# A hybrid decoder layer on one core: split weight pieces of the input projection kept in DRAM between its two passes

## The chip, the cores and the metric

The kernel runs on one core of one Trainium2 chip. The metric is the device time of one execution in microseconds (us); a version's time is the median of several executions. A profile is one execution with the hardware profiler on. Engines are named as in its rows: PE is TensorE (matmuls; PEld its weight loads), DVE is VectorE, ACT is ScalarE, POOL is GpSimd, and SP is the engine whose in-order queue issues the DMA transfers. The granted clock (PEclk) is given in parts of TensorE's full speed, 2.4 GHz.

## The reference, cut to what matters

One layer over a sequence of 2048 tokens with 1024 features. All of x is normalised and multiplied by one matrix `w_in` of 1024 x 4096; its columns feed three groups of heads, whose outputs are concatenated, multiplied by `w_out` (1536 x 1024), normalised and added to x.

```python
hn = rms_norm(x, g_pre)
proj = hn @ w_in                                  # (2048, 1024) @ (1024, 4096)
rg_x, rg_g, da_q, da_k, da_v, da_g, xa_q, xa_g = jnp.split(proj, cuts, axis=-1)

xc = causal_depthwise_conv(rg_x, conv_w, conv_b)  # width 4 along the sequence
y_rg = rg_lru(xc, w_rg_a, b_rg_a, w_rg_x, b_rg_x, lru_lambda) * silu(rg_g)

o = diff_attention(q, k, v, lam)                  # 4 heads, causal, two softmaxes each
y_da = rms_norm(o, g_subln) * (1.0 - LAMBDA_INIT) * silu(da_g)

km, vm = split(rms_norm(mem, g_mem) @ w_mem_kv)   # 256 memory tokens
y_xa = mem_cross_attention(xa_q, km, vm) * silu(xa_g)

y = concatenate([y_rg, y_da, y_xa]) @ w_out
x = x + rms_norm(y, g_post)
```

## The kernel before

Everything is fp32. For its matmuls a tensor is split into a high part (the value rounded to a matmul format) and a low part (what the rounding left), and each product is three matmuls: high x high, low x high, high x low (`mm3`). A weight is split by `split_weight`: ACT casts the raw piece to the high half (L237), then POOL subtracts that from the raw piece to get the low half (L238).

**The projection.** The sequence is cut into four chunks of 512 tokens, and the 4096 columns of `w_in` into 16 pairs of 256 (`PAIRS`): `qk` (query and key of a head), `v`, `g` (gates), `xa` (memory attention) and `rg` (the recurrent group). `project()` runs twice. The first pass goes over chunks 0 and 1, the second over chunks 2 and 3 with the pairs in the order `ORDER_B`. A pair has four steps u, one for each chunk and half of the pair; a step is a sum of 24 matmuls over 8 blocks kb of the contraction. The `ip` tiles of the profile are the results of these steps.

**The weight pieces.** The weight of a pair comes in four pieces, each for two blocks kb: raw 128 x 512 (256 KB, `wraw`), split 128 x 1024 (512 KB, `wp`). Raw pieces have three buffers, split ones six (`pw`). Pieces are numbered in the order of use: 0 to 7 and 24 to 79 for the first pass, 8 to 23 for the memory tokens' weight `w_mem`, 80 to 143 for the second pass. `w_load(i)` issues the transfer of a raw piece on SP (L316), `w_conv(i)` splits it and issues `w_load(i + 3)`. While a pair runs, `project()` converts the first two pieces of the next pair in its steps 0 and 1, and the other two in step 3, after the blocks 1 and 3, since each of these takes over the buffer of a piece whose last matmul has just been given out. So in the second pass all of `w_in` is read and split once more.

**The rest.** The queries, keys, values and gates of the attention go through DRAM: `ev_qk` and its like store them (`QD`, `KD`, `VD`, `GD`), and the attention loads them back (`q` L645, `kv` L608 and L621, `gt` L775). The softmax streams run between the projection's matmuls; in them DVE and POOL scale the exponentials `e` by the row sums (L719, L718), PE transposes the result (`pt`), and ACT and DVE split it (`pthl`, L759, L760). The group outputs wait in DRAM (`YD`) for the output projection (`po`). For an `rg` pair, `ev_rg` runs the convolution on DVE (`xc`, L550, L553), casts it to a high half (`xchl`, L556, DVE) and subtracts for the low half (L557, POOL); the gates' matmuls (`rgo`) read both. Then `rg_gates` runs the recurrence (a scan on DVE, L590).

**What sets the order.** PE's order is written out by the program: a clock of its own (`now`, `pump`, `spawn`) hands out the attention's matmuls between those of the projection. DVE, ACT and POOL get their order from a scheduler with priorities. SP's queue is in order: an issue that waits for its buffer or its data holds every later one back. `store(fn, delay)` spawns an issue that much later on the program's own clock.

Of the kernel before, what the change touches and what calls it, by code (L numbers as in the profile page):

```python
# [9 lines left out]
F32 = mybir.dt.float32  # L10
# [39 lines left out]
ORDER_B = (0, 12, 2, 13, 1, 14, 3, 15, 4, 8, 6, 9, 7, 10, 11, 5)  # L50
# [7 lines left out]
def hybrid_layer(  # L58
# [13 lines left out]
    nc = tc.nc  # L72
# [14 lines left out]
    dr = ctx.enter_context(tc.tile_pool(name="dr", bufs=1, space=bass.MemoryType.DRAM))  # L87

    def f4(name, shape=(128, 1024), dt=F32, pool=p4):
        return pool.tile(list(shape), dt, tag="f4", name=name)  # L90
# [19 lines left out]
    def asf(ap):  # L110
        return ap.bitcast(F32)
# [4 lines left out]
    KD = [[dr.tile([2, 2, 64, CH], F32, name=f"KD{h}{c}") for c in range(NCH)] for h in range(4)]  # L116
    VD = [[dr.tile([128, 2, 4, 128], F32, name=f"VD{h}{c}") for c in range(NCH)] for h in range(4)]
    GD = [[dr.tile([128, CH], F32, name=f"GD{h}{c}") for c in range(NCH)] for h in range(4)]
    KMD = dr.tile([4, 128, 1024], F32, name="KMD")
    YD = [[dr.tile([4, 128, 4, 128], F32, name=f"YD{g}{c}") for c in range(NCH)] for g in range(3)]  # L120

# [82 lines left out]
    def spawn(gen, delay=0.0):  # L204
        streams.append([now[0] + delay, gen])

    def store(fn, delay):

        def go():
            fn()  # L210
            return
            yield
        spawn(go(), delay)
# [22 lines left out]
    def split_weight(raw, hi, lo, eng=nc.gpsimd):  # L236
        nc.scalar.copy(hi, raw)  # L237
        eng.tensor_sub(lo, raw, asf(hi))  # L238
# [65 lines left out]
    def pair_pieces(ps):  # L304
        return [w_in[4 * p + i] for p in ps for i in range(4)]

    wsrc = (pair_pieces(range(2)) + [w_mem[i] for i in range(16)] + pair_pieces(range(2, 16))
            + pair_pieces(ORDER_B))
    MEM0 = 8
    wraw, wcv = {}, {}  # L310

    def w_load(*ids):
        for i in ids:
            if i < len(wsrc):
                wraw[i] = praw.tile([128, 512], F32, tag="raw", name="wraw")
                nc.sync.dma_start(wraw[i], wsrc[i])  # L316

    def w_conv(*ids, eng=nc.gpsimd, pool=pw):
        for i in ids:
            if i < len(wsrc) and i not in wcv:  # L320
                w = wcv[i] = f4("wp", (128, 2, 2, 256), F32R, pool)
                split_weight(wraw.pop(i), w[:, 0].rearrange("p a b -> p (a b)"),
                             w[:, 1].rearrange("p a b -> p (a b)"), eng)
                w_load(i + 3)


    def load_rows(src, n, name):
# [21 lines left out]
    stored = set()  # L349
    setup()  # L350
    w_load(0)
    xr0 = load_rows(x, 4, "xrow")
    w_load(1, 2)
    xb = bigt("xrows", (128, 4, 2, 512), F32)
    xr1 = [[xb[:, i, j, :] for j in range(2)] for i in range(4)]
# [3 lines left out]
    for row in xr0:  # L359
        norm_rows([row], nc.vector)  # L360
    w_conv(0, eng=nc.vector)
    new_hnT(0)
    for _ in transpose_norm(xr0, hnT[0], V_GPRE):
        pass
    ready.add(0)
    w_conv(1, 2, 3, eng=nc.vector)

    def prep_mem():
# [9 lines left out]
    def store_km(i, ts):  # L378
        for j, t in enumerate(ts):
            nc.sync.dma_start(KMD[i + j], asf(t).rearrange("p a b -> p (a b)"))  # L380

    def memory_branch():
# [6 lines left out]
        for p in range(4):  # L389
            i0 = MEM0 + 4 * p  # L390
            if p == 2:
                vmh = f4("vmh", (128, 2, 512), F32R)
                vml = f4("vml", (128, 2, 512), F32R)
            for half in range(2):
                o = ps_m("kv", (128, 256))
                for kb in range(KB):
                    w = wcv[i0 + kb // 2]
                    if p < 2:
                        cs = slice(half * 128, half * 128 + 128)
                        mm3(o, w[:, 0, kb % 2, cs], w[:, 1, kb % 2, cs],  # L400
                            memT[0][:, kb, :], memT[1][:, kb, :], kb == 0, kb == KB - 1)
                    else:
                        tk = slice(half * 128, half * 128 + 128)
                        mm3(o, memT[0][:, kb, tk], memT[1][:, kb, tk], w[:, 0, kb % 2, :], w[:, 1, kb % 2, :],
                            kb == 0, kb == KB - 1)
                    if half == 1 and kb in (1, 3):
                        w_conv(i0 + 6 + kb // 2, eng=nc.vector if kb == 1 else nc.gpsimd)
                    pump()
                if p < 2:
                    hi, lo = kmh[:, 2 * p + half, :], kml[:, 2 * p + half, :]  # L410
                else:
                    cs = slice((p - 2) * 256, (p - 2) * 256 + 256)
                    hi, lo = vmh[:, half, cs], vml[:, half, cs]
                nc.scalar.copy(hi, o)
                nc.vector.tensor_sub(lo, o, asf(hi))
                if half == 0:
                    w_conv(i0 + 4, eng=nc.vector)
                    w_conv(i0 + 5)
                elif p % 2:
                    store(lambda i=p - 1, ts=(kmh, kml) if p == 1 else (vmh, vml): store_km(i, ts), 4.0)  # L420
# [34 lines left out]
    def ev_g(hp, c, half, o):  # L455
        t = f2("gs", (128, CH))
        sigmoid(t, o)
        nc.vector.tensor_mul(t, o, t)
        store(lambda: nc.sync.dma_start(GD[2 * hp + half][c], t), 4.0)

# [4 lines left out]
    def load_km():  # L465
        for i, n in enumerate(("kmh", "kml", "vmh", "vml")):
            t = state[n] = f4(n, (128, 4, 256) if i < 2 else (128, 2, 512), F32R)
            nc.sync.dma_start(asf(t).rearrange("p a b -> p (a b)"), KMD[i])

# [256 lines left out]
    def t_stream(jobs):  # L726

        for h, pr in jobs:
# [45 lines left out]
            c, j = divmod(pr, 2)  # L774
            nc.sync.dma_start(gt, GD[h][c][:, j * 256:j * 256 + 256])  # L775
            nc.scalar.copy(A[:, 0, :], o)
# [23 lines left out]
    def project(chunks, i0, order, hooks, head=False):  # L800
# [5 lines left out]
        for p, u in steps:  # L806
# [27 lines left out]
            for t, kb, ot, wh, wl, xh, xl in mms:  # L834
                mm3(ot, wh, wl, xh, xl, kb == 0, kb == KB - 1)
                if u == 3 and t == (kind == "v"):
                    if first:
                        if kb % 2 and (p == 0 or kb < 4):
                            w_conv(MEM0 + 4 * p + kb // 2)
                    elif kb in (1, 3):  # L840
# [209 lines left out]
```

## Time and profile before

| | |
|---|---|
| median of 3 runs | 1487.29 us (1485.58 to 1488.57) |
| profiled execution | 1490.95 us, its span 1489.1 us |
| busy in the span | PE 95%, PEld 81%, DVE 62%, ACT 54%, POOL 38% |
| mean granted clock | 0.986 |
| SP's DMA queue | 182.64 MB |
| largest group of PE | `ip` matmuls, 676.8 us for the 128x512 form |

The span is counted from the profiled execution's first instruction to its last; its own time is 1.85 us more than that. The busy shares are means over stages. By the first and last instructions of the `ip` groups, the first pass lies at about 0 to 540 us, the second at 540 to 1106, and the output projection after it.

### The profile page before, as it was taken

To read this page: it belongs to the slowest core of one execution; us is meant where nothing else is said; L and a number is where in the kernel's file an instruction comes from. 1 tells how busy PE (TensorE), PEld (TensorE's weight loads), DVE (VectorE), ACT (ScalarE), POOL (GpSimd) and SP (SyncE) were. 2 spreads that over 40 slices of the span, in tenths; PEclk is the share of its full clock that TensorE was granted. 3 is DMA by queue.
4 is the path that set the end of the run, shared out by engine and by line. 5 is a ranking of instruction groups with operands and counts; after the bars stand their busy time and mean duration, and the time that the engine had idled before them with its cause. 6 is when DMAs were issued, how large, how long until landed. Compare 5 with 4: busy or idle time off the path is not lost.

```text
span 1489.1 us, 21951 instructions
## 1 busy us (share of the span) xinstructions
PE 1422.1 (95%) x7568; PEld 1208.6 (81%) x7568; DVE 918.4 (62%) x1862; ACT 811.5 (54%) x1972; POOL 563.8 (38%) x634
## 2 busy tenths in 40 slices
PE   5999999999998899899998999999999999999997
PEld 4789889888886678787786898888877888888886
DVE  6332565677545776757648576767778777777222
ACT  6343545666458674755556555666566545554221
POOL 2231433443446543535425343423346433334221
PEclk9999999999999899999999999999999999999999
DMA  6666666342322146244222543221375234322231
GB/s 218 162 214 219 177 172 206 99 132 82 106 68 64 50 128 187 72 151 123 84 68 71 163 141 128 68 85 40 116 237 174 86 133 151 103 96 76 99 123 70
DMA packets 138655, 184.05 MB, mean 124 GB/s; under 512 B 11440, under 2 KB 81200, under 8 KB 138544
## 3 DMA queue, kind: packets, MB, share of 16 engines
q1 hardware_dynamic: 138400, 182.64, 39.6%
q8 instruction: 59, 0.97, 0.3%
q14 instruction: 52, 0.43, 0.1%
q10 hardware_dynamic: 144, 0.01, 0.0%
HBM read 125.99 MB, written 56.62 MB: 123 GB/s over the span
## 4 chain that ended last, share of the span: by engine, by line
PE 74%; DVE 8%; ACT 6%; POOL 5%; issue 4%; DMA 2%; SPq 0%; DVEq 0%; POOLq 0%; ACTq 0%
PE ip L197 35%; PE po L197 17%; PE s L197 7%; PE o L197 6%; PE pt L201 4%; DVE e L719 2%; PE xas L197 2%; PE kv L197 1%; POOL e L718 1%; PE xao L197 1%; POOL wp L238 1%; DMA wraw<-in_w_in_dram 1%; PE rgo L197 1%; DVE xc L553 1%; ACT e L695 1%
## 5 line engine op out<-in xcount | busy, mean ns | idle before, releaser
L197 PE MATMUL ip<-hnT,wp 128*128 128x512 f32 x2688 | 676.8, 397 | 4.9 <-DVE rgg L563 4.9
L197 PEld LDWEIGHTS ip<-hnT,wp 128*128 128x128 f32 x2688 | 499.0, 190 | 105.8 <-DVE rgg L563 6.1
L695 ACT ACTIVATE e<-s,nm 128x512 f32<-128x512 f32 (+3 forms) x320 | 200.0, 625 | 233.4 <-DVE nm L693 216.3
L238 POOL TENSOR_TENSOR wp<-wraw,wp 128x512 fp32r<-128x512 f32 x133 | 182.2, 1380 | 201.8 <-ACT wp L237 192.8
L693 DVE TENSOR_REDUCE nm<-s 128x1 f32<-128x512 f32 (+3 forms) x320 | 193.2, 605 | 32.4 <-PE s L197 27.7
L197 PE MATMUL po<-wout,yg 128*128 128x512 f32 x768 | 193.5, 393 | 4.2 <-POOL wout L238 1.9
L718 POOL TENSOR_SCALAR e<-e,f 128x512 f32<-128x512 f32 (+3 forms) x160 | 120.3, 767 | 171.1 <-DVE f L714 93.5
L197 PE MATMUL s<-kv,q 128*128 128x512 f32 (+3 forms) x640 | 182.8, 367 | 1.0 <-ACT e L695 0.9
L197 PEld LDWEIGHTS po<-wout,yg 128*128 128x128 f32 x768 | 141.3, 188 | 34.3 <-POOL wout L238 3.3
L719 DVE SCALAR_TENSOR_TENSOR e<-e,f 128x512 f32<-128x512 f32 (+3 forms) x160 | 142.7, 919 | 28.5 <-POOL e L718 28.3
L197 PE MATMUL o<-pthl,kv 128*128 128x256 f32 (+1 forms) x864 | 136.3, 293 | 2.0 <-DVE pthl L760 2.0
L760 DVE TENSOR_TENSOR pthl<-pt,pthl 128x512 fp32r<-128x512 f32 (+1 forms) x144 | 94.6, 657 | 70.4 <-ACT pthl L759 70.0
L197 PEld LDWEIGHTS s<-kv,q 128*128 128x128 f32 x640 | 114.6, 189 | 21.8 <-ACT e L695 1.3
L197 PEld LDWEIGHTS o<-pthl,kv 128*128 128x128 f32 x864 | 116.1, 192 | 5.6 <-DVE pthl L760 2.8
L238 POOL TENSOR_TENSOR yg<-yraw,yg 128x512 fp32r<-128x512 f32 x48 | 64.2, 1341 | 133.1 <-ACT yg L237 122.0
L237 ACT CAST wp<-wraw 128x512 fp32r<-128x512 f32 x144 | 88.2, 618 | 43.9 <-PE ip L197 22.1
L759 ACT CAST pthl<-pt 128x512 fp32r<-128x512 f32 (+1 forms) x144 | 80.8, 561 | 53.3 <-PE pt L201 52.7
L197 PE MATMUL ip<-wp,hnT 128*128 128x256 f32 x768 | 99.4, 284 | 0.0
L197 PE MATMUL po<-wo,yg 128*128 128x512 f32 x384 | 97.3, 392 | 0.0
L197 PEld LDWEIGHTS ip<-wp,hnT 128*128 128x128 f32 x768 | 96.2, 192 | 1.2
L201 PE MATMUL pt<-ident,e 128*128 128x128 f32 x544 | 84.4, 276 | 5.6 <-DVE pthl L760 5.6
L201 PEld LDWEIGHTS pt<-ident,e 128*128 128x128 f32 x544 | 67.9, 142 | 20.8 <-DVE pthl L760 6.0
(183 smaller groups left out, 1731.2 us busy)
## 6 DMA issues: line engine op xcount, KB each, us to landing
wraw<-in_w_in_dram SPq DMA_DIRECT2D x128, 256.0 KB, 2.7
q<-QD SPq DMA_DIRECT2D x128, 128.0 KB, 3.3
kv<-KD SPq DMA_DIRECT2D x24, 512.0 KB, 5.7
kv<-VD SPq DMA_DIRECT2D x24, 512.0 KB, 5.0
yraw<-YD SPq DMA_DIRECT2D x48, 256.0 KB, 2.7
QD<-qkhl SPq DMA_DIRECT2D x32, 256.0 KB, 3.3
KD<-qkhl SPq DMA_DIRECT2D x32, 256.0 KB, 3.7
VD<-vhl SPq DMA_DIRECT2D x32, 256.0 KB, 2.8
```

Of the source, the lines that this page charges most:

```text
L197: nc.tensor.matmul(o, w, xx, start=start, stop=stop)
L201: nc.tensor.transpose(o, i, ident)
L237: nc.scalar.copy(hi, raw)
L238: eng.tensor_sub(lo, raw, asf(hi))
L553: nc.vector.scalar_tensor_tensor(xc[:, 0:CH], xr[:, k:k + CH], vec2[:, cw + k:cw + k + 1], xc[:, 0:CH], op0=ALU.mult, op1=ALU.add)
L693: nc.vector.tensor_reduce(out=nm[:, c, kc:kc + 1], in_=s[:, 0:w], op=ALU.max, axis=AX.X, negate=True)
L695: nc.scalar.activation(e[kc, c][:, 0:w], s[:, 0:w], AF.Exp, bias=nm[:, c, kc:kc + 1], accum_out=l[:, c, kc:kc + 1])
L718: nc.gpsimd.tensor_scalar(e2, e2, f[:, 1, kc:kc + 1], 1.0, op0=ALU.mult, op1=ALU.mult)
L719: nc.vector.scalar_tensor_tensor(e1, e1, f[:, 0, kc:kc + 1], e2, op0=ALU.mult, op1=ALU.add)
L759: nc.scalar.copy(hi[:, 0:n], t[:, 0:n])
L760: nc.vector.tensor_sub(lo[:, 0:n], t[:, 0:n], asf(hi[:, 0:n]))
```

## The change

In the first pass each of the 64 pieces of `w_in` is stored to a DRAM tile `WD` after it is split (512 KB, L333 of the changed kernel). In the second pass `w_conv` loads that tile into the `wp` buffer with one transfer (512 KB, L326); there is no raw transfer, no cast and no subtraction. The pieces of `w_mem` are not stored, since they are used once. The new lines shift the line numbers by up to 10.

```diff
--- before.py
+++ after.py
@@ -116,6 +116,7 @@
     KD = [[dr.tile([2, 2, 64, CH], F32, name=f"KD{h}{c}") for c in range(NCH)] for h in range(4)]
     VD = [[dr.tile([128, 2, 4, 128], F32, name=f"VD{h}{c}") for c in range(NCH)] for h in range(4)]
     GD = [[dr.tile([128, CH], F32, name=f"GD{h}{c}") for c in range(NCH)] for h in range(4)]
+    WD = [[dr.tile([128, 1024], F32, name=f"WD{p}{i}") for i in range(4)] for p in range(16)]
     KMD = dr.tile([4, 128, 1024], F32, name="KMD")
     YD = [[dr.tile([4, 128, 4, 128], F32, name=f"YD{g}{c}") for c in range(NCH)] for g in range(3)]
 
@@ -306,12 +307,12 @@
 
     wsrc = (pair_pieces(range(2)) + [w_mem[i] for i in range(16)] + pair_pieces(range(2, 16))
             + pair_pieces(ORDER_B))
-    MEM0 = 8
+    MEM0, WB0 = 8, 80
     wraw, wcv = {}, {}
 
     def w_load(*ids):
         for i in ids:
-            if i < len(wsrc):
+            if i < WB0:
                 wraw[i] = praw.tile([128, 512], F32, tag="raw", name="wraw")
                 nc.sync.dma_start(wraw[i], wsrc[i])
 
@@ -319,9 +320,18 @@
         for i in ids:
             if i < len(wsrc) and i not in wcv:
                 w = wcv[i] = f4("wp", (128, 2, 2, 256), F32R, pool)
+                if i >= WB0:
+
+                    q = ORDER_B[(i - WB0) // 4]
+                    nc.sync.dma_start(asf(w).rearrange("p a b c -> p (a b c)"), WD[q][i % 4])
+                    continue
                 split_weight(wraw.pop(i), w[:, 0].rearrange("p a b -> p (a b)"),
                              w[:, 1].rearrange("p a b -> p (a b)"), eng)
                 w_load(i + 3)
+                if not MEM0 <= i < MEM0 + 16:
+                    q = i if i < MEM0 else i - 16
+                    store(lambda w=w, q=q: nc.sync.dma_start(
+                        WD[q // 4][q % 4], asf(w).rearrange("p a b c -> p (a b c)")), 4.0)
 
 
     def load_rows(src, n, name):
```

PE's order is the same in both kernels. DVE's and ACT's lists differ in small shifts, beside ACT's casts that are gone. Three places show what moves.

GpSimd, at the second `rg` pair of the second pass, before the change: its list from the copy that begins the convolution on.

```order
L544 COPY xr<-halo 128x3
L718 TENSOR_SCALAR e<-e,f 128x512
L718 TENSOR_SCALAR e<-e,f 128x256
L238 TENSOR_TENSOR wp<-wraw,wp 128x512 x3
L557 TENSOR_TENSOR xchl<-xc,xchl 128x512
L238 TENSOR_TENSOR wp<-wraw,wp 128x512
L584 TENSOR_TENSOR ri<-ri,xc 128x512
```

The same place after the change.

```order
L554 COPY xr<-halo 128x3
L728 TENSOR_SCALAR e<-e,f 128x512
L728 TENSOR_SCALAR e<-e,f 128x256
L567 TENSOR_TENSOR xchl<-xc,xchl 128x512
L599 TENSOR_TENSOR ri<-ri 128x512
L602 COPY carry<-ri 128x1
L594 TENSOR_TENSOR ri<-ri,xc 128x512
```

The four subtractions `wp`, three of them ahead of `xchl`, are gone; the subtraction of `xchl` follows directly on the scaling of `e`.

SP, in the second pass, at the handover from the `qk` pair of head 1 to the next `rg` pair, before the change (`q` are loads for the attention, `YD` stores of results).

```order
L645 DMA q_6896<-QD_100 128x2x128 x2
L795 DMA YD_168<-oa 128x2x128
L645 DMA q_7070<-QD_100 128x2x128 x2
L316 DMA wraw<-in_w_in_dram 128x512 x3
L462 DMA YD_165<-ri 128x4x128
L316 DMA wraw<-in_w_in_dram 128x512
L645 DMA q_7248<-QD_100 128x2x128
```

The same place after the change.

```order
L655 DMA q_6967<-QD_100 128x2x128 x2
L805 DMA YD_232<-oa 128x2x128
L326 DMA wp<-WD_168 128x1024
L655 DMA q_7132<-QD_100 128x2x128
L326 DMA wp<-WD_169 128x1024
L655 DMA q_7132<-QD_100 128x2x128
L326 DMA wp<-WD_218 128x1024
L326 DMA wp<-WD_219 128x1024
L472 DMA YD_229<-ri 128x4x128
L655 DMA q_7304<-QD_100 128x2x128
```

The four raw loads are four loads of the double size, which stand one by one where the split stood in the program.

SP, in the first pass, where the attention of head 0 begins, before the change.

```order
L316 DMA wraw<-in_w_in_dram 128x512 x3
L645 DMA q_1628<-QD_98 128x2x128 x2
L645 DMA q_1686<-QD_99 128x2x128 x2
L775 DMA gt<-GD_146 128x256
L316 DMA wraw<-in_w_in_dram 128x512
L459 DMA GD_151<-gs 128x512
L440 DMA QD_106<-qkhl 64x512
L438 DMA QD_106<-qkhl 64x2x512 x2
L440 DMA QD_106<-qkhl 64x512
L645 DMA q_1767<-QD_99 128x2x128 x2
L645 DMA q_1907<-QD_99 128x2x128 x2
```

The same place after the change.

```order
L655 DMA q_1711<-QD_98 128x2x128 x2
L333 DMA WD_181<-wp 128x1024
L317 DMA wraw<-in_w_in_dram 128x512
L469 DMA GD_151<-gs 128x512
L655 DMA q_1770<-QD_99 128x2x128 x2
L785 DMA gt<-GD_146 128x256
L333 DMA WD_182<-wp 128x1024
L448 DMA QD_106<-qkhl 64x2x512
L450 DMA QD_106<-qkhl 64x512
L448 DMA QD_106<-qkhl 64x2x512
L450 DMA QD_106<-qkhl 64x512
L317 DMA wraw<-in_w_in_dram 128x512
```

Stores of 512 KB (`WD`) stand between the raw loads and the loads of `q`.

## Rows read from the trace of the kernel before

**Rows 1.** Windows: busy us of PE, PEld, DVE, ACT, POOL; clock; DMA share; GB/s.

```profile
100.00:250.00 150.00, 148.72 (x916) 133.31 (x915) 70.86 (x164) 66.54 (x161) 49.72 (x53) 1.00 0.64 190
540.00:1106.00 566.00, 545.96 (x2964) 465.60 (x2963) 379.79 (x722) 334.58 (x797) 227.85 (x253) 0.98 0.38 115
1106.00:1489.00 383.00, 370.59 (x1880) 310.84 (x1878) 234.44 (x509) 173.96 (x460) 134.77 (x130) 0.99 0.36 119
```

**Rows 2.** TensorE's waits, 500 to 1106 us; total, times, longest.

```profile
PE rgo L197 <- POOL xchl L557: 6.7, 4, 2.3
PE pt L201 <- DVE pthl L760: 5.6, 1, 5.6
PE rgo L197 <- DVE xchl L556: 3.0, 3, 1.1
...
PE rgo L197 <- ACT e L695: 0.4, 1, 0.4
```

**Rows 3.** GpSimd's and ScalarE's groups by shape, 504 to 1106 us.

```profile
L238 POOL TENSOR_TENSOR wp<-wraw,wp 128x512 fp32r<-128x512 f32 x66 | 92.1, 1405 | 85.5 <-ACT wp L237 79.0 <-PE xao L197 3.7 <-DMA wraw<-in_w_in_dram 2.5
...
L237 ACT CAST wp<-wraw 128x512 fp32r<-128x512 f32 x65 | 39.9, 619 | 14.7 <-PE ip L197 11.7 <-DMA wraw<-in_w_in_dram 2.4 <-POOL xr L544 0.4
```

**Rows 4.** GpSimd's timeline, 596 to 614 us; start, duration, instruction, [idle before <-releaser].

```profile
603.63 3.43 POOL L238 TENSOR_TENSOR wp<-wraw,wp 128x512 fp32r<-128x512 f32 x2
609.61 1.85 POOL L238 TENSOR_TENSOR wp<-wraw,wp 128x512 fp32r<-128x512 f32 x1 [2.55 <-DMA wraw<-in_w_in_dram]
611.42 1.26 POOL L557 TENSOR_TENSOR xchl<-xc,xchl 128x512 fp32r<-128x512 f32 x1
```

**Rows 5.** VectorE's timeline of the same stretch.

```profile
605.83 1.78 DVE L553 SCALAR_TENSOR_TENSOR xc<-xr,vec,xc 128x512 f32<-128x512 f32 x1
...
609.19 0.41 DVE L556 CAST xchl<-xc 128x512 fp32r<-128x512 f32 x1
```

**Rows 6.** VectorE's L553 over the whole span; ns min/median/max.

```profile
L553 DVE SCALAR_TENSOR_TENSOR xc<-xr,vec,xc x48: 720/752/1853, 428.0 to 797.3; 128x512 f32<-128x512 f32 x48
```

**Rows 7.** VectorE's and GpSimd's timelines, 786 to 797 us.

```profile
789.06 2.31 DVE L590 TENSOR_TENSOR_SCAN ri<-rga,carry,ri 128x512 f32<-128x512 f32 x1
...
791.87 1.51 DVE L553 SCALAR_TENSOR_TENSOR xc<-xr,vec,xc 128x512 f32<-128x512 f32 x1
793.31 1.75 DVE L593 TENSOR_TENSOR ri<-ri,rgg 128x512 f32<-128x512 f32 x1
...
791.57 4.61 POOL L238 TENSOR_TENSOR wp<-wraw,wp 128x512 fp32r<-128x512 f32 x3
```

**Rows 8.** TensorE's timeline, 505 to 520 us, and 749 to 762 us.

```profile
513.19 1.22 PE L197 MATMUL rgo<-xchl,rgh 128*128 128x512 f32 x2 [2.21 <-POOL xchl L557]
...
515.06 5.25 PE L197 MATMUL ip<-hnT,wp 128*128 128x512 f32 x14
...
748.83 12.86 PE L197 MATMUL ip<-hnT,wp 128*128 128x512 f32 x56
```

**Rows 9.** Windows of four us around the stall at 789 us.

```profile
793.00:797.00 4.00, 1.28 (x6) 1.28 (x7) 4.00 (x5) 1.78 (x5) 3.19 (x2) 0.50 0.56 153
797.00:801.00 4.00, 4.00 (x18) 3.33 (x17) 3.70 (x7) 2.51 (x6) 1.29 (x1) 0.75 0.42 109
```

**Rows 10.** The DMA queue of SP over the whole execution.

```profile
q1 hardware_dynamic: 138400, 182.64, 39.6%
```

**Rows 11.** DMA issues by line; KB each, median us from issue to landing.

```profile
xres<-in_x_dram SPq DMA_DIRECT2D x16, 512.0 KB, 3.7
...
kv<-KD SPq DMA_DIRECT2D x24, 512.0 KB, 5.7
...
vml<-KMD SPq DMA_DIRECT2D x2, 512.0 KB, 6.7
KMD<-kmh SPq DMA_DIRECT2D x1, 512.0 KB, 4.0
```

**Rows 12.** Waits of SP's queue, 540 to 1130 us.

```profile
SPq L316 <- POOL wp L238: 173.4, 49, 29.1
```

## The prediction

> **What bounds the kernel now.** I read the busy time by stage first, then what TensorE waits for in the stage that the change rewrites, then the timelines of the engines at the longest of these waits. In the second pass TensorE is busy for 545.96 of 566 us, in the output projection for 370.59 of 383 [rows 1]. So TensorE's own work is the bound, and that the change doesn't touch: its order is the same. All that can be won lies in the gaps of the second pass and in the clock behind them. Between 500 and 1106 us ten rows of waits sum to 24.1 us, from 6.7 us down to 0.4 [rows 2]: 9.7 us of them are the gates' matmuls `rgo` waiting for the two halves of `xchl`, 5.6 us one wait of a transpose on VectorE's `pthl`, and 8.8 us the seven others. None of the ten names a weight piece: the split is always in time for the matmuls that read it. It costs TensorE something only through its place in the lists of other engines.
>
> **What is removed.** From the second pass go the POOL subtractions of 1.405 us and the ACT casts of 0.619 us [rows 3]. For 64 pieces that is 64 x 1.405 = 90 us of POOL and 64 x 0.619 = 40 us of ACT. POOL is busy for 228 us of 566 there, ACT for 335 [rows 1]: neither is the bound, so these 130 us are worth nothing as they stand. What counts is what stood behind them.
>
> *Subtractions ahead of `xchl`.* At 608 us POOL's list has three of them ahead of the subtraction for `xchl`. The third waits 2.55 us for its raw transfer, starts at 609.61 and holds `xchl` until 611.42, though VectorE's cast, its input, ended at 609.19 + 0.41 = 609.60 [rows 4, 5]. Without it `xchl` starts 1.8 us earlier. One step before, VectorE's L553 took 1.78 us beside POOL's work where its median is 0.752 [rows 5, 6]; if it takes its median, the cast comes 1.0 us earlier as well. Together 2.8 us of the 1.13 + 2.30 = 3.43 us that TensorE lost there; I take 0.82 of such a place. At 508 us the wait is of the same kind (2.21 us of it on `xchl` [rows 8]), but of the two subtractions ahead one belongs to the last piece of the first pass and stays, so I take half of 3.3 us, 1.7. The other places hold 9.7 - 3.3 = 6.4 us, at 0.82 of them 5.2. Sum **6.9 us**. Bounds: 3.5, if only the direct step of 1.8 us at 608 and 1.7 us at 508 is won, and 9.7.
>
> *VectorE's stretched instructions.* At 789 us VectorE's scan L590 takes 2.31 us, L553 1.51 and L593 1.75, and a run of three POOL subtractions lies beside them [rows 7]; `pthl` stands behind them. L553 has a median of 0.752, so it lost 0.76 us [rows 6]; if the other two were stretched by about the same share, a half, they lost 1.16 and 0.88. Together **2.8 us** of the 5.6. Bounds: 0, if the length is due to other POOL work (more of it stands there), and 5.6. Beside this I weigh a rule: the Trainium skill, SBUF — State Buffer, section Who interferes with whom, says that a VectorE instruction with two SBUF inputs contends with a GpSimd instruction that reads SBUF, and that the loser blocks for as long as the other runs. The spread of L553, 0.720 to 1.853 us, agrees with it [rows 6]. By the rule the whole stretch would go with the subtractions, and the sum would be the same 2.8 us here.
>
> *The clock.* After such a stall the granted clock stands at 0.50 for a while, as in the window behind the wait at 789 us, and at 0.75 in the next one [rows 9]; 0.50 is the lower of its two levels, 1.2 GHz. Behind the stall at 508 us 14 projection matmuls take 5.25 us, 0.375 each, where 56 take 12.86, 0.230 each, in an undisturbed stretch [rows 8]: 14 x 0.145 = 2.0 us a stall. Three more stalls (two of the other `rgo` waits and the one at 789 us) should shrink to near nothing; I take half of 3 x 2.0, **3.0 us**. Bounds 0 and 8 (four stalls).
>
> *The other waits*, 24.1 - 9.7 - 5.6 = 8.8 us. They stand on VectorE and ACT, which have less beside them and less in their lists. No row says how much; I take a third, **2.9 us**. Bounds 0 and 8.8.
>
> Sum of gains 6.9 + 2.8 + 3.0 + 2.9 = 15.6 us; bounds 3.5 and 32.
>
> **What is added.** *Stores in the first pass.* 64 x 512 KB = 33.6 MB. The queue moved 182.64 MB in 39.6% of the span [rows 10], so 0.396 x 1489.1 = 590 us of all 16 engines, 310 GB/s: the stores cost 108 us of them, 0.20 of the 540 us of that pass. Its densest part, 100 to 250 us, has 0.64 now, with TensorE busy for 148.72 of 150 us [rows 1]. 0.84 leaves room, but the loads of `q` and of the raw pieces stand behind stores in SP's queue, and each landing gets longer. A store of this size landed in 4.0 us [rows 11]; it holds its `wp` buffer so much longer. I take **1.5 us**; bounds 0 and 6 (three places that each wait half a store, 2 us).
>
> *Loads in the second pass.* 33.6 MB in place of 16.8: 54 us more of the 16 engines, so 0.38 + 54/566 = 0.48 of them, no bound [rows 1, 10]. What has to be weighed is lateness. A piece's buffer comes free in step 3 of a pair, and the piece is needed in step 0 of the next: between lie 18 matmuls of the one and 12 of the other, 30 x 0.230 = 6.9 us from [rows 8], plus the attention's matmuls between them. The split before took its raw data from a load made ahead; now the whole transfer must land within that time. 512 KB landed in 3.7 us (`xres`), 5.7 (`kv`) and 6.7 (`vml`, one of four loads issued together) [rows 11]. A load that is alone is nearest to `xres`, one behind `q` and `kv` loads nearest to `kv`; both are under 6.9. A `v` pair has narrower matmuls at its end and leaves less. I take **1.0 us**; bounds 0 and 7 (rival 2). SP's waits themselves are no loss: it waited 173.4 us for the subtractions before, in 49 waits [rows 12], and now waits for TensorE to leave the buffers, with the same stores and `q` loads behind it.
>
> The output projection keeps its order on TensorE, and its weights are split as before, so nothing is taken there.
>
> **Sum.** 15.6 - 1.5 - 1.0 = 13.1 us less than the profiled execution's 1490.95: 1477.9. That execution is 3.66 us above the median of the runs, 1487.29, which makes **1474.2 us**, 0.9% faster. Differences under 0.2%, 3 us, a measurement of this kernel can hardly tell from none.
>
> **The rivals.**
>
> 1. *The waits only move.* Each list keeps its order, and a wait of TensorE on `xchl` ends when the convolution on VectorE ends. If VectorE is late by itself (its cast was the last in 3.0 us of the waits [rows 2]), or another POOL instruction takes the place of the subtraction, only the direct 3.5 us remain, and 2.5 us of costs against them: -1 us, 1486.3. Against it: the third subtraction at 608 us started after its raw transfer, not after VectorE [rows 4]. Chance 0.12, as "same", 1484 to 1490.
>
> 2. *The loads land late (slower).* Place: the handovers between the 16 pairs. If a load lands 8 us after its buffer came free, TensorE waits about 1 us at each handover without attention matmuls between, say six of them: 6 us, and the gain halves to 1480. It decides between faster and slower where 15 handovers cost 15 us, with a landing of 6.9 + 1.0 = 7.9 us at all of them, or near 9.5 at six; then the time would be 1490 to 1500. For it: 6.7 us for `vml` is within 0.2 of the margin, and the DMA share rises. Against it: the same row is one of four loads together, and single ones land in 3.7 [rows 11]. Chance 0.08. A page speaks to this: the Trainium skill, DMA: Bandwidth & Descriptors, section Latency and other measured facts, gives 0.2 us on average for an HBM access and 2 us at high load; an estimate from it, 3.7 + 1.8 = 5.5 us, would still leave no wait and the sum as above. The trace of before can't show which of the two holds for these loads.
>
> 3. *The first pass pays for the stores.* With 0.84 of the DMA engines taken between 100 and 250 us, each `q` and `kv` load behind a store comes later by a store's 4.0 us [rows 11]; four such waits of TensorE, with one fall of the clock of 2.0 us each [rows 8], cost 24 us against 15.6: 1495. It decides from about 2.6 such waits on. Against it: the loads are issued ahead of their use, and TensorE hardly waits there now [rows 1]. Chance 0.05.
>
> 4. *More goes than the waits show.* Nearly all of the 24.1 us and the clock's 8: 1464 or less. Chance 0.05.
>
> **How the numbers follow.** My forecast has 0.70, with its own range 1466 to 1482 (gains of 8 to 24 less 2.5 us of costs, from 1487.29). The range for 8 in 10 reaches to 1464 below, where 23 of the possible 32 us are won, and to 1486 above, where only the direct steps and the small costs are left. Faster by over 0.2%: the forecast, the fourth rival and a part of the second, 0.78. Within 0.2%: 0.10. Slower: 0.12, from rivals 2 and 3 and the worse part of 1.
>
> **What the profile after would show.** If I am right: no wait of `rgo` on `xchl` over 1 us behind 600 us, about 1.7 us left at 508, L553 near its median throughout the second pass, the wait at 789 us halved, clock windows of 0.50 only at the start of the second pass; a landing of `wp` loads of 4 to 5.7 us, and of the first pass a length within 2 us of the present one. I'd be wrong if TensorE waits for `wp` at handovers (rival 2), if the first pass is longer by over 5 us (rival 3), or if the `rgo` waits stay with VectorE as the releaser (rival 1).

## The result

| | before | after |
|---|---|---|
| median of four runs | 1486.43 us (1485.5 to 1488.57) | 1470.62 us (1470.07 to 1470.96) |
| ratio | | 0.9891, 95% interval 0.9874 to 0.9908 |
| profiled execution, its span | 1490.95, 1489.1 | 1470.07, 1468.3 |

The changed kernel is 1.1% faster, 15.8 us in the median; 1474.2 was predicted. The two profiled executions are 20.9 us apart, since that of before lay 4.5 us above its median and that of after 0.6 below. What follows is read from these two.

The busy times first, with the number of instructions behind the x: before, then the changed kernel.

```profile
PE 1422.1 (95%) x7568; PEld 1208.6 (81%) x7568; DVE 918.4 (62%) x1862; ACT 811.5 (54%) x1972; POOL 563.8 (38%) x634
PE 1411.8 (96%) x7568; PEld 1202.1 (82%) x7568; DVE 899.6 (61%) x1862; ACT 777.6 (53%) x1908; POOL 476.8 (32%) x570
```

TensorE runs the same 7568 matmuls and is busy for 1411.8 us, where it was 1422.1: 10.3 us less for the same work. VectorE runs the same 1862 instructions in 899.6 us in place of 918.4: 18.8 us less, though the change takes nothing from it. That second number turns out to be the story. Three of VectorE's groups over the whole kernel (busy us, mean ns of one), before:

```profile
L719 DVE SCALAR_TENSOR_TENSOR e<-e,f 128x512 f32<-128x512 f32 (+3 forms) x160 | 142.7, 919 | 28.5 <-POOL e L718 28.3
L760 DVE TENSOR_TENSOR pthl<-pt,pthl 128x512 fp32r<-128x512 f32 (+1 forms) x144 | 94.6, 657 | 70.4 <-ACT pthl L759 70.0
L553 DVE SCALAR_TENSOR_TENSOR xc<-xr,vec,xc 128x512 f32<-128x512 f32 x48 | 49.6, 1033 | 1.0
```

and after:

```profile
L729 DVE SCALAR_TENSOR_TENSOR e<-e,f 128x512 f32<-128x512 f32 (+3 forms) x160 | 137.8, 886 | 29.7 <-POOL e L728 29.4
L770 DVE TENSOR_TENSOR pthl<-pt,pthl 128x512 fp32r<-128x512 f32 (+1 forms) x144 | 94.4, 656 | 69.0 <-ACT pthl L769 68.5
L563 DVE SCALAR_TENSOR_TENSOR xc<-xr,vec,xc 128x512 f32<-128x512 f32 x48 | 43.4, 904 | 1.0
```

The convolution's steps (L553) give 6.2 of the 18.8 us and the scaling of `e` (L719) 4.9, while `pthl`, which reads a result of TensorE, stays as it was.

Windows of the changed kernel, with the columns of [rows 1].

```profile
100.00:250.00 150.00, 146.81 (x905) 131.12 (x904) 69.26 (x162) 66.17 (x159) 49.70 (x52) 1.00 0.82 264
540.00:1106.00 566.00, 554.21 (x3036) 473.85 (x3035) 371.12 (x743) 316.85 (x768) 156.42 (x199) 1.00 0.48 153
```

In the dense part of the first pass the DMA share went from 0.64 to 0.82 and TensorE lost 1.9 us of its 150. Between 540 and 1106 us GpSimd fell from 228 to 156 us (the second pass ends earlier now, so the window holds 21 us of the output projection).

TensorE's waits from 500 us to the end of the second pass, which now ends near 1085 us.

```profile
PE pt L202 <- DVE pthl L770: 3.3, 1, 3.3
PE rgo L198 <- POOL xchl L567: 2.1, 3, 1.2
PE xt L202 <- DVE hnT L299: 1.1, 1, 1.1
PE rgo L198 <- DVE xchl L566: 1.1, 1, 1.1
...
PE s L198 <- ACT xap L512: 0.2, 1, 0.2
```

All eight rows sum to 9.9 us; it was 24.1 [rows 2]. `rgo` waits 3.2 us in place of 9.7, `pt` 3.3 in place of 5.6. No matmul waits for a loaded weight piece.

GpSimd and VectorE at the second `rg` pair, the place of [rows 4, 5].

```profile
605.40 1.80 POOL L567 TENSOR_TENSOR xchl<-xc,xchl 128x512 fp32r<-128x512 f32 x1 [3.94 <-DVE xchl L566]
```

```profile
601.03 0.96 DVE L563 SCALAR_TENSOR_TENSOR xc<-xr,vec,xc 128x512 f32<-128x512 f32 x1
...
602.58 0.74 DVE L563 SCALAR_TENSOR_TENSOR xc<-xr,vec,xc 128x512 f32<-128x512 f32 x1
...
603.84 0.74 DVE L563 SCALAR_TENSOR_TENSOR xc<-xr,vec,xc 128x512 f32<-128x512 f32 x1
...
604.90 0.41 DVE L566 CAST xchl<-xc 128x512 fp32r<-128x512 f32 x1
```

GpSimd's subtraction for `xchl` now follows the cast on VectorE, not a weight piece. But the cast comes earlier as well: the convolution's second step took 0.74 us where it took 1.78. At 789 us before, 776 now, the same is to be seen on the scan and its neighbours:

```profile
775.39 1.27 DVE L600 TENSOR_TENSOR_SCAN ri<-rga,carry,ri 128x512 f32<-128x512 f32 x1
...
777.17 0.73 DVE L563 SCALAR_TENSOR_TENSOR xc<-xr,vec,xc 128x512 f32<-128x512 f32 x1
777.83 0.68 DVE L603 TENSOR_TENSOR ri<-ri,rgg 128x512 f32<-128x512 f32 x1
```

2.31, 1.51 and 1.75 us [rows 7] became 1.27, 0.73 and 0.68. TensorE still waits 3.3 us there, and in the window behind it the granted clock (the number ahead of the DMA share) is still low:

```profile
780.00:784.00 4.00, 4.00 (x17) 3.53 (x17) 2.61 (x6) 2.14 (x6) 1.28 (x1) 0.57 0.48 158
```

The transfers, KB each and median us to landing.

```profile
WD<-wp SPq DMA_DIRECT2D x64, 512.0 KB, 4.6
wp<-WD SPq DMA_DIRECT2D x64, 512.0 KB, 4.4
...
q<-QD SPq DMA_DIRECT2D x128, 128.0 KB, 3.6
```

The new loads land in 4.4 us in the median, well under the 6.9 us of the handover. The only wait of TensorE on a transfer in the first pass is one `q` load behind stores, at 148 us:

```profile
PE s L198 <- DMA q<-QD: 1.5, 1, 1.5
```

TensorE runs the same matmuls in the same order in every kernel of this document, so the start of the n-th one can be compared between two profiles. The table gives how much later (+) or earlier (-) than in the kernel before it starts, in us; matmul 2500 is near the end of the first pass, 5500 near that of the second, 7567 is the last. The kernels after the first are those of the experiments.

| kernel | 500 | 1500 | 2500 | 3500 | 4500 | 5500 | 7567 |
|---|---|---|---|---|---|---|---|
| the change | +1.0 | +3.4 | +3.4 | -9.9 | -17.4 | -20.2 | -20.8 |
| stores only (e1) | +0.5 | +2.5 | +4.1 | +1.9 | +2.5 | +2.4 | +2.8 |
| loads only (e2) | -2.5 | -2.5 | -2.5 | -16.2 | -23.2 | -25.9 | -27.0 |
| low halves (e4) | -0.6 | -0.5 | -0.5 | -14.7 | -20.7 | -22.9 | -22.9 |
| high halves, subtraction kept (e5) | -1.1 | -1.1 | -1.2 | -7.6 | -6.7 | -8.1 | -9.5 |
| memset in its place (e6) | +0.1 | 0.0 | 0.0 | -4.6 | -11.7 | -14.6 | -15.5 |
| subtraction on VectorE (e11) | +0.5 | +0.5 | +0.5 | -11.8 | -19.4 | -19.4 | -19.7 |

The change loses 3.4 us by matmul 1500, 2.4 of them between 500 and 1500 in the dense part of the first pass, and wins 23.6 between 2500 and 5500; the output projection is 0.6 us shorter.

### The profile page after: what moved, and what is told of

Same layout as the page of the kernel before. It is cut to its first block, busy times and chain, and to the rows that moved or that the text cites. A ratio compares the mean times of both kernels' runs of the same rounds, so it can differ in the third digit from the quotient of the medians.

```text
span 1468.3 us, 21840 instructions
## 1 busy us (share of the span) xinstructions
PE 1411.8 (96%) x7568; PEld 1202.1 (82%) x7568; DVE 899.6 (61%) x1862; ACT 777.6 (53%) x1908; POOL 476.8 (32%) x570
## 4 chain that ended last, share of the span: by engine, by line
PE 74%; DVE 8%; ACT 6%; DMA 4%; issue 4%; POOL 3%; SPq 1%; DVEq 0%; ACTq 0%; POOLq 0%
PE ip L198 35%; PE po L198 17%; PE s L198 7%; PE o L198 6%; PE pt L202 3%; PE xas L198 1%; DMA q<-QD 1%; DVE xc L563 1%; PE xao L198 1%; DVE e L729 1%; PE rgo L198 1%; DVE nm L703 1%; PE xt L202 1%; PE xat L202 1%; ACT ri L260 1%
## 5 line engine op out<-in xcount | busy, mean ns | idle before, releaser
L729 DVE SCALAR_TENSOR_TENSOR e<-e,f 128x512 f32<-128x512 f32 (+3 forms) x160 | 137.8, 886 | 29.7 <-POOL e L728 29.4
L198 PEld LDWEIGHTS s<-kv,q 128*128 128x128 f32 x640 | 114.5, 189 | 23.6 <-DMA q<-QD 2.0
L239 POOL TENSOR_TENSOR wp<-wraw,wp 128x512 fp32r<-128x512 f32 x69 | 93.4, 1363 | 120.8 <-ACT wp L238 108.8
L198 PEld LDWEIGHTS po<-wo,yg 128*128 128x128 f32 x384 | 70.9, 188 | 14.2
```

Source lines behind the costliest of these rows:

```text
L198: nc.tensor.matmul(o, w, xx, start=start, stop=stop)
L729: nc.vector.scalar_tensor_tensor(e1, e1, f[:, 0, kc:kc + 1], e2, op0=ALU.mult, op1=ALU.add)
```

## The experiments

All times are medians, the ratio is to the kernel before run on the same chip, with its 95% interval.

| run | median us | ratio |
|---|---|---|
| e1, stores only | 1493.10 | 1.0030 (1.0014 to 1.0046) |
| e2, loads only | 1463.63 | 0.9839 (0.9816 to 0.9863) |
| e3, the split put back beside the change | 1507.41 | 1.0126 (1.0103 to 1.0149) |
| e4, low halves through DRAM | 1468.28 | 0.9862 (0.9840 to 0.9885) |
| e5, high halves through DRAM, subtraction kept | 1483.16 | 0.9980 (0.9967 to 0.9992) |
| e6, memsets in place of the subtraction | 1472.58 | 0.9908 (0.9892 to 0.9924) |
| e7, each piece loaded twice | 1498.56 | 1.0078 (1.0059 to 1.0096) |
| e8, before with `xchl` on VectorE | 1484.85 | 0.9988 (0.9978 to 0.9997) |
| e9, e4 with `xchl` on VectorE | 1467.46 | 0.9873 (0.9856 to 0.9890) |
| e10, e4 with the first pass's subtractions on VectorE | 1468.81 | 0.9880 (0.9865 to 0.9894) |
| e11, before with the second pass's subtractions on VectorE | 1470.57 | 0.9892 (0.9878 to 0.9907) |
| e12, the same for 36 of 64 pieces | 1472.87 | 0.9906 (0.9889 to 0.9923) |

**What do stores and loads cost? e1 and e2.** The changed kernel with the second pass of before:

```diff
-            if i < WB0:
+            if i < len(wsrc):
...
-                if i >= WB0:
...
-                    nc.sync.dma_start(asf(w).rearrange("p a b c -> p (a b c)"), WD[q][i % 4])
-                    continue
...
-                if not MEM0 <= i < MEM0 + 16:
+                if i < WB0 and not MEM0 <= i < MEM0 + 16:
```

> The 64 stores of the first pass are added; the second pass loads raw pieces and splits them as before. Matched matmul by matmul, the trace of the changed kernel loses 4.4 us in the first pass against the one of before and wins about 24 in the second. If the loss is the price of the stores, this kernel is 4 us slower than before (1488 to 1493 against 1486.4) and loses nothing in the second pass. Rival: the loss came from the other order of the first pass (the raw loads of the second pass no longer prefetched behind it) and the stores cost nothing: 1485 to 1488.

Measured 1.0030, 4.5 us slower (2.1 to 6.8): the stores' price, in the first pass as the table shows. And the loads without the stores:

```diff
-                    nc.sync.dma_start(asf(w).rearrange("p a b c -> p (a b c)"), WD[q][i % 4])
+                    nc.sync.dma_start(asf(w).rearrange("p a b c -> p (a b c)"), WD[0][i % 4])
...
-                if not MEM0 <= i < MEM0 + 16:
+                if i < 4:
```

> Only the four pieces of the first pair are stored, and every piece of the second pass is loaded from these four tiles, so that the second pass uses wrong weights but moves the same bytes: the loads without the stores. If the stores cost 4.4 us, 1465 to 1468 against 1470.6 of the changed kernel, with a first pass as long as before. Rival: the stores cost nothing, 1469 to 1472.

Its ratio is 0.0052 under that of the change, 7.7 us, more than expected, but with an interval of some 4 us to either side. The profiles are 6.2 us apart, nearly all of it in the first pass; 2.5 us of these e2 is ahead of the kernel before as well by matmul 500, for which its four stores give no reason. So what the stores took is a few us: 3.4 by the profiles of before and after, 4.5 and 7.7 by the runs.

**Which removed work was it? e4 and e5.** Half of each piece goes through DRAM, the other half is made as before. In e4 the low half is loaded and ACT casts the high one:

```diff
...
+                    nc.sync.dma_start(asf(w[:, 1]).rearrange("p b c -> p (b c)"), WD[q][i % 4])
+                    nc.scalar.copy(w[:, 0].rearrange("p a b -> p (a b)"), wraw.pop(i))
+                    w_load(i + 3)
```

> Only the low halves are stored and loaded (256 KB each way); the second pass loads the raw piece as before and casts the high half on ACT. It removes GpSimd's subtractions and keeps ACT's casts, and halves the stores. If the subtractions are the cause and half the stores cost half: 4.4 / 2 = 2.2 us less than the changed kernel, 1467 to 1470. Rival: the removed casts carried part of the gain: 1473 to 1482. Were they all of it, 1484 to 1489.

In e5 the high half is loaded and GpSimd subtracts the raw piece from itself, so that no subtraction waits for a cast or a load of `WD`; the low halves are zero:

```diff
...
+                    nc.sync.dma_start(asf(w[:, 0]).rearrange("p b c -> p (b c)"), WD[q][i % 4])
+                    r, lo = wraw.pop(i), w[:, 1].rearrange("p a b -> p (a b)")
+                    eng.tensor_sub(lo, r, r)
+                    w_load(i + 3)
```

> The counterpart of the run with the low halves: the high halves are stored and loaded (256 KB each way), ACT's casts are gone, and GpSimd subtracts for the low half as before (the raw piece from itself, so that it need not wait for the load: the second pass has low halves of zero). Its list has three subtractions ahead of xchl at the second rg pair. If the subtractions are the cause, the gain is gone: 1483 to 1491, with L553 at 0.95 to 1.0 us in the mean and the rgo waits of before. Rival: the casts on ACT are the cause: 1466 to 1474.

e4 has the whole gain with all 64 casts still on ACT; e5, without the casts, is only 0.2% faster than before. So the subtractions are the cause, and the casts can be worth no more than a few us, a size that no run shows by itself. Half the stores cost little: in e4 matmul 2500 starts 0.5 us earlier than before, 2.0 later than in e2. Its ratio is below that of the change, but the intervals overlap.

**How does a subtraction cost? e6.** Two ways were open: it stands in GpSimd's list ahead of others, or it holds VectorE up. In place of e5's subtraction stand two memsets, which write the same half and read nothing:

```diff
-                    eng.tensor_sub(lo, r, r)
+                    eng.memset(asf(lo), 0.0)
+                    eng.memset(asf(lo), 0.0)
```

> As the run before, with two memsets of the low half on GpSimd in place of the subtraction: they only write, and are meant to take about as long together (1.0 to 1.3 us). Two ways in which a subtraction can cost something are told apart. If it is its place in GpSimd's list ahead of xchl and e, this run loses what the run with the subtractions loses, within 4 us. If it is that VectorE's instructions with two inputs in SBUF are held up by a GpSimd instruction that reads, L553 is back at 0.75 to 0.80 us and half or more of the gain is back: 1470 to 1479.

The groups by shape in the second pass, busy us and mean ns, for e5 (VectorE's convolution, then GpSimd's subtraction):

```profile
L566 DVE SCALAR_TENSOR_TENSOR xc<-xr,vec,xc 128x512 f32<-128x512 f32 x24 | 23.5, 981 | 0.4
```

```profile
L328 POOL TENSOR_TENSOR wp<-wraw 128x512 fp32r<-128x512 f32 x64 | 74.7, 1175 | 76.3 <-PE ip L198 73.1 <-issue 2.7 <-PE pt L202 0.5
```

and for e6:

```profile
L567 DVE SCALAR_TENSOR_TENSOR xc<-xr,vec,xc 128x512 f32<-128x512 f32 x24 | 18.6, 775 | 0.4
```

```profile
L329 POOL MEMSET wp<- 128x512 f32 x64 | 34.7, 543 | 3.2
L328 POOL MEMSET wp<- 128x512 f32 x64 | 33.5, 525 | 72.3 <-PE ip L198 72.2
```

GpSimd is nearly as busy for a piece in the one as in the other, 0.525 + 0.543 = 1.07 us against 1.175 (before, a subtraction took 1.405). VectorE's convolution step takes 0.775 us beside the memsets and 0.981 beside the subtractions, and the time is 1472.6 against 1483.2: 0.0072 of the ratio, 10.7 us. Over the whole page VectorE is busy for 916.4 us in e5 and 896.4 in e6, with the same instructions:

```profile
PE 1415.7 (96%) x7568; PEld 1204.4 (81%) x7568; DVE 916.4 (62%) x1862; ACT 777.3 (53%) x1908; POOL 552.5 (37%) x634
```

```profile
PE 1415.1 (96%) x7568; PEld 1205.3 (82%) x7568; DVE 896.4 (61%) x1862; ACT 778.0 (53%) x1908; POOL 540.4 (37%) x698
```

At the second `rg` pair e6 has six memsets ahead of `xchl`, and they are through before VectorE's cast has begun:

```profile
604.03 0.52 POOL L328 MEMSET wp<- 128x512 f32 x1
...
606.72 0.52 POOL L329 MEMSET wp<- 128x512 f32 x1
608.41 1.77 POOL L571 TENSOR_TENSOR xchl<-xc,xchl 128x512 fp32r<-128x512 f32 x1 [1.17 <-DVE xchl L570]
```

```profile
605.59 0.74 DVE L567 SCALAR_TENSOR_TENSOR xc<-xr,vec,xc 128x512 f32<-128x512 f32 x1
...
607.91 0.41 DVE L570 CAST xchl<-xc 128x512 fp32r<-128x512 f32 x1
```

In e5 three subtractions stand ahead of `xchl` at this place, and they too are through before the cast, which they made late (the convolution's step at 601.00 us took 1.52 us):

```profile
598.05 3.93 POOL L328 TENSOR_TENSOR wp<-wraw 128x512 fp32r<-128x512 f32 x3
604.60 1.77 POOL L570 TENSOR_TENSOR xchl<-xc,xchl 128x512 fp32r<-128x512 f32 x1 [2.62 <-DVE xchl L569]
```

So in both runs `xchl` waits for VectorE there and not for its place in the list; the subtraction, which reads, held VectorE up, and the memsets, which only write, did not. The Trainium skill, SBUF — State Buffer, section Who interferes with whom, which the prediction weighed, has the same distinction: a VectorE instruction with two SBUF inputs contends with a GpSimd instruction that reads SBUF, and not with one that only writes it. The 0.981 and 0.775 us agree with it.

e6 is still 0.0046 of the ratio behind e4, 4 to 7 us. That need not be the place in the list: since nothing reads the raw pieces in e6, their loads run ahead in SP's queue (all are issued by 620 us), and TensorE has two waits on transfers that e4 and e5 don't have, 5.7 us together:

```profile
PE s L198 <- DMA kv<-KD: 3.8, 1, 3.8
...
PE ip L198 <- DMA wp<-WD: 1.9, 1, 1.9
```

The early raw loads are no rival for e6's gain: e4 and e11 load theirs in step with the splitting and are at least as fast.

**The list alone: e8.** Before, with one edit that frees `xchl` from GpSimd's list and leaves all 64 subtractions:

```diff
-            nc.gpsimd.tensor_sub(xh[:, 1], xc[:, 0:CH], asf(xh[:, 0]))
+            nc.vector.tensor_sub(xh[:, 1], xc[:, 0:CH], asf(xh[:, 0]))
```

> The kernel before, with only the low half of xchl subtracted on VectorE and not on GpSimd, so that it stands behind no weight piece; no store, no change of the loads. If the place in GpSimd's list is what cost most, the 6.7 us of rgo waits and some of the clock behind them come back: 1474 to 1481 against 1487.7. If VectorE's held-up instructions cost most, they stay, and VectorE has 16 x 0.7 = 11 us more to do: 1484 to 1490.

0.9988, 0.4 to 3.3 us faster, at the lower end of the rival. TensorE's waits of e8 from 500 to 1106 us:

```profile
PE pt L201 <- DVE pthl L760: 5.7, 1, 5.7
PE ip L197 <- DVE rgg L563: 3.9, 4, 1.3
...
PE rgo L197 <- DVE xchl L557: 1.9, 3, 1.0
PE rgo L197 <- DVE xchl L556: 1.8, 2, 1.4
```

The waits on GpSimd's `xchl` are gone, but `rgo` waits on VectorE for it, and 3.9 us of `ip` on VectorE's `rgg` are new: TensorE meets the next late result of the same engine. The edit acts on both passes, and at 481 us, at the end of the first, `rgo` waits 6.1 us for VectorE's subtraction; so the 0.1% is net of what VectorE's added work costs, not the price of the list alone.

**Without DRAM: e11 and e12.** If reading on GpSimd is the cause, the subtraction can stay on the chip and move to VectorE. The kernel before, with nothing but this:

```diff
-                             w[:, 1].rearrange("p a b -> p (a b)"), eng)
+                             w[:, 1].rearrange("p a b -> p (a b)"), nc.vector if i >= 80 else eng)
```

> The kernel before with the second pass's 64 subtractions on VectorE (0.7 us each) in place of GpSimd; nothing goes through DRAM. GpSimd reads nothing for them, so VectorE's instructions with two inputs are no longer held up, but 64 x 0.7 = 45 us stand in VectorE's list. If the hold-up is the cause and 45 us fit into VectorE's idle time: 1472 to 1480. Rival: the subtractions now stand in VectorE's list ahead of what TensorE waits for, as they did in GpSimd's: 1482 to 1492.

```profile
L238 DVE TENSOR_TENSOR wp<-wraw,wp 128x512 fp32r<-128x512 f32 x58 | 41.6, 721 | 11.7 <-ACT wp L237 11.5
...
L553 DVE SCALAR_TENSOR_TENSOR xc<-xr,vec,xc 128x512 f32<-128x512 f32 x24 | 18.8, 782 | 0.3
```

1470.57 us, ratio 0.9892: the gain of the change (0.9891) without a byte of split weight through DRAM. VectorE does its 0.72 us a piece, and its convolution steps take 0.782 us. In e12 `80 <= i < 116` stands in the condition.

> The kernel before with the subtractions of 36 of the 64 pieces of the second pass on VectorE: those that are split while its first eight pairs run, among which are the four rg pairs; the other 28 stay on GpSimd. If a held-up VectorE costs only where the convolution and the scan run, nearly the whole gain of all 64 is there, 1470 to 1474. Rival: it costs wherever the softmax scales e on VectorE, so that the gain goes with the number of pieces, 36 of 64 of 16.5 us: 1476 to 1480.

14.0 us of e11's 16.5 come with 36 of the 64 pieces, not the 9.3 that their number would give: most is lost while the first eight pairs run, the four `rg` pairs and four others. That it is the `rg` pairs among them isn't shown apart. The other 28 pieces are left with about 2.5 us, under what this measurement can tell.

**How near are the loads to being late? e7.** Each load twice, one after the other:

```diff
                     nc.sync.dma_start(asf(w).rearrange("p a b c -> p (a b c)"), WD[q][i % 4])
+                    nc.sync.dma_start(asf(w).rearrange("p a b c -> p (a b c)"), WD[q][i % 4])
```

> The changed kernel with each load of a split piece issued twice in a row into the same buffer, the second after the first has landed: a landing of about 9 us in place of 4.4, which is over the 6.9 us that lie between the release of a buffer and its use. If the margin is as I counted it, TensorE waits about 2 us at the handovers that have no attention matmuls between: 1480 to 1495, with waits of ip on wp in the trace. Rival: the attention's matmuls between give room for that too: 1470 to 1474.

```profile
PE ip L198 <- DMA wp<-WD: 13.9, 13, 3.2
```

```profile
PE 1426.6 (95%) x7568; PEld 1209.1 (81%) x7568; DVE 899.4 (60%) x1862; ACT 778.3 (52%) x1908; POOL 476.5 (32%) x570
```

13 waits of 1.1 us in the mean, half as long as expected. Still the kernel is 28 us slower than the change, past the range: in the second pass (matmuls 2570 to 5689) TensorE's gaps are 16.8 us longer than in the changed kernel, the 13.9 us among them, and its matmuls are busy for 10.0 us more. A wait cost about 1.6 times its length. The rest of the 14.8 us by which the page's PE is above that of the change lies in stretches in which no load is doubled.

**Inconclusive, and without effect: e3, e9, e10.** e3 put raw load, cast and subtraction back beside the change, in place in the raw buffer.

```diff
...
+                    r = wraw.pop(i)
+                    nc.scalar.copy(r.bitcast(F32R), r)
+                    eng.tensor_sub(r.bitcast(F32R), r, r)
+                    w_load(i + 3)
```

> The changed kernel with the work that it removed put back beside it: the raw load, an ACT cast and a GpSimd subtraction for each piece of the second pass, made in place in the raw buffer, whose result nobody reads. GpSimd's list has its three subtractions ahead of xchl again at the second rg pair. If the gain is the removed engine work's place in the lists, it goes: the second pass is as long as before, 1486 to 1494. Rival: the gain came from the weight's path itself (the load goes straight to the buffer, no chain of raw load, cast and subtraction in front of the matmuls); then 1470 to 1474.

It was slower than anything foreseen, and not for the reason under test. The casts no longer wait for a buffer but for their raw piece, which stands in SP's queue behind a load that waits for a buffer, and they hold ACT's list meanwhile:

```profile
ACT wraw L328 <- DMA wraw<-in_w_in_dram: 21.0, 15, 3.1
```

The run tells nothing about the split, and e4 to e6 were built to keep the place of the work without this wait. e9 (e4 with e8's edit) and e10 (e4 with `nc.vector if i >= 24 else eng` for the first pass) tried to win more.

> The run with the low halves, with xchl's low half subtracted on VectorE as well. 3.0 us of rgo waits on GpSimd's xchl are left in that run's second pass, and more in the first; VectorE gets 16 x 0.7 us more. If the last reads of GpSimd beside the convolution still hold VectorE up, 1462 to 1467 against 1468.3. Rival: VectorE's own queue takes back what GpSimd's gives, 1467 to 1472.

> The run with the low halves, with the first pass's subtractions for the pieces of w_in after the memory tokens' on VectorE in place of GpSimd: 56 x 0.7 us more for VectorE, 56 x 1.4 us less for GpSimd. The waits that are left between 400 and 540 us stand on VectorE and on xchl beside such subtractions. If the hold-up costs there what it cost in the second pass, 1461 to 1467. Rival: VectorE's longer list costs as much, 1467 to 1475.

Both fall on the rival's side and can't be told from e4. So three kernels lie at 0.986 to 0.988, none shown to be faster than another, and e4's step under the change isn't shown either.

## Why the prediction was right, point by point

The forecast, 1474.2, was 3.6 us above the result, and the sign and the range held. That it came so near is in part luck. Against the profiled executions, from which the sum starts, I was 7.8 us off (1477.9 for 1470.07): that of before lay 4.5 us above its median by the four runs, that of after 0.6 below. And the sum hides terms that were off by more.

1. **The cause** was GpSimd's subtractions and not ACT's casts: shown by e4, e5 and e11.
2. **"Subtractions ahead of `xchl`", 6.9 us.** The `rgo` waits fell by 6.5 us, so the size was right. At 608 us before, `xchl` starts 3.8 us earlier against the matmuls around it (shifted by 2.2 us at that point): 1.7 us because nothing stands before it, where I had 1.8, and 2.0 because the cast is earlier, where I had 1.0. So the half that goes through VectorE was the larger one. Freeing `xchl` from the list, at VectorE's expense, was worth 0.1% (e8).
3. **"VectorE's stretched instructions", 2.8 us.** The three instructions that I had looked at became 1.04, 0.78 and 1.07 us shorter, 2.9 in all, and the wait of 5.6 us shrank by 2.3: there the term was right. (The three subtractions of [rows 7] begin behind the scan; beside the scan ran a fourth, of 1.47 us at 788.82.) What failed is the place given to the hold-up: I priced it at this one wait. But it acted on many more of VectorE's instructions: 18.8 us of its busy time over the kernel, and 10.7 us of the kernel's (e6 against e5), so that part of the other terms is its work. Nor is it in two-input instructions alone: 2.6 of the 18.8 us are those of L586 (11.2 us before, 8.6 after), which has one tile as input. I had written that by the rule of the Trainium skill (SBUF — State Buffer, section Who interferes with whom) the sum would be "the same 2.8 us here"; read over the whole pass, what goes with the reading is 10.7 of the 15.8 us.
4. **"The clock", 3.0 us, at most 8.** This term was mis-sized most. Between the matmuls that start at 500 and at 1106 us of before (numbers 2570 and 5689) TensorE's matmuls are busy for 574.1 us where they were busy for 582.1: 8.0 us less, my upper bound. The four stalls that I had counted are the ones with a low clock behind them in that stretch, and no short one has it. Ten us at two of them, 611 and 789 us, before (the clock stands ahead of the DMA share):

```profile
610.00:620.00 10.00, 7.70 (x36) 6.81 (x36) 4.95 (x11) 8.07 (x18) 4.16 (x4) 0.66 0.34 106
790.00:800.00 10.00, 4.42 (x18) 3.83 (x18) 9.85 (x12) 4.77 (x11) 6.34 (x6) 0.66 0.46 132
```

and after:

```profile
604.00:614.00 10.00, 9.59 (x70) 8.68 (x69) 7.75 (x15) 9.17 (x19) 3.69 (x4) 1.00 0.39 124
777.00:787.00 10.00, 7.18 (x36) 6.38 (x37) 6.64 (x12) 7.16 (x17) 1.28 (x1) 0.83 0.31 98
```

At the other two, from 511 us (the stall that I put at 508) and from 731 (719 after), 0.66 and 0.83 became 0.83 and 1.00. Ten us at 0.66 cost matmuls that run through them 3.4 us, at 0.83 1.7: 11.9 us in the four before, 3.4 after. My 2.0 us a stall came from 14 `ip` matmuls and left out the slow `rgo` matmuls ahead of them [rows 8]; and two of the four went wholly, two by half, where I took half of three. The length of a stall does not settle what follows it: behind the same wait of 2.9 us near 485 us, ahead of the second pass, ten us stand at 0.66 before and at 0.83 after. The other 2.3 of TensorE's 10.3 us lie there and in the output projection, and nothing in the change accounts for them.
5. **"The other waits", 2.9 us.** All waits fell by 14.2 us; less 6.5 and 2.3, 5.4 us are these.
6. **Stores, 1.5 us, at most 6.** 3.4 us by the profiles, 4.5 (e1) or 7.7 (e2 against the change) by the runs: the right place, but under half of the size. Rival 3's mechanism was there, with one wait on a `q` load of 1.5 us out of the 2.4 us of the dense part; 1.0 us was lost before matmul 500, where a wait of 1.2 us on `kml` in the memory tokens' part is new.
7. **Loads, 1.0 us.** None: no wait, a landing of 4.4 us in the median, nearer to the single 512 KB load (3.7) than to `kv` (5.7). Single loads took up to 8.7 us without a wait of TensorE. In e7 two landings, 4.9 and 4.8 us in the median, make 9.7; with my margin of 6.9 that would be waits of 2.8 us where they were 1.1 in the mean, so the margin of rival 2 is, as an estimate from these numbers, nearer to 8.6.

Rival 1 did not come true: `rgo` waits 1.1 us on VectorE's cast where it waited 3.0. Between matmuls 2500 and 5500 the gain was 23.6 us where I had 15.6, and the cost ahead of it 3.4 where I had 2.5. Why that one execution of before was 4.5 us slower than its median is open; so is how the 10.7 us between e5 and e6 divide over VectorE's instructions, which was not tried apart.

## What to carry to other kernels

Before work is taken off GpSimd for the time it takes, look at what VectorE's own instructions cost beside it: a line whose mean (here 1033 ns) or longest time (1853) lies well above its median (752), with a reading GpSimd instruction beside the long ones, shows a hold-up that no busy share and no wait names. Then the cheapest cure is to move the reader, not to remove the work: here 64 subtractions on VectorE (0.72 us each) gave the same time as 33.6 MB of stores and as much of loads. And where TensorE is the bound, price a wait by its length and the slow matmuls behind it; here that was about 1.6 times the length, both when waits went (14.1 us of gaps and 8.0 of matmul time) and when they came (16.8 and 10.0 in e7).

## What I had not expected of the hardware

- Two memsets of GpSimd, 1.07 us together, left the mean of VectorE's convolution step at 0.775 us, where one subtraction of 1.175 us, which reads, brought it to 0.981.
- VectorE's same 1862 instructions took 2% less, 899.6 us for 918.4, when 64 subtractions left another engine.
- In e7 16.8 us of added waits, 13.9 of them in 13 waits of 1.1 us, came with 10.0 us of added matmul time.
